# Attention by blocks of sixteen query columns in a two-layer diffusion trunk

## The chip, the cores and the metric

The kernel runs on one core of one Trainium2 chip. The metric is the device time of one execution in microseconds; for the kernel before it is the median of three runs. One execution was also taken by the hardware profiler, and the views quoted below come from that one.

## What is computed

The reference is a two-layer trunk over 256 latent tokens (a grid of 4 rows and 64 columns) with 256 context tokens, width 1024. What matters here is the attention of each layer, with 8 heads of 64 channels:

```python
# per latent query at grid column c, all 4 rows are in reach (kh = min(8, rows) = 4)
col_start = jnp.clip(cols - 8, 0, 64 - 16)          # a window of 16 columns
s_win = q . k_window * scale + bias                 # 4 x 16 = 64 window keys
s_ctx = q . k_ctx * scale                           # 256 context keys
p = softmax(concat([s_win, s_ctx]))                 # one softmax over both
out = p_win @ v_window + p_ctx @ v_ctx
```

So a latent query sees 64 of the 256 latent keys, and all 256 context keys. q and k are turned by a rotary table first. Context tokens attend to context only, in the first layer; the last layer needs only their keys and values. The rest of a layer is an input projection (convolution branch, q/k/v, gates), a depthwise convolution of 31 taps, output projections and a gated MLP with 2816 channels.

## The kernel before

**Products.** Activations are held with channels on the 128 partitions and tokens along the free axis: 256 latent tokens, then 256 context tokens (slices `LAT`, `CTX`). A weight unit of 128 x 1024 floats comes from HBM by a DMA that SP issues (`raw_unit`, L146; tag `raw`, four buffers). It is split into a high and a low fp32r half: ACT casts the high half (L161), and DVE subtracts for the low half (L162); for the units in `ADDED`, ACT makes the high half and its negative (L199, L200) and a DMA that GpSimd issues adds the raw unit to it (L201). A product is then three fp32r matmuls (`mm3`, L180 to L182). A *group* is one output tile of 128 channels: 8 input chunks times three matmuls of 512 columns in layer 0 and of 256 in layer 1.

**Attention.** Layer 0 first makes V for its four token tiles of 128 (`v_tile`, L683) and copies each from its PSUM bank (L816); layer 1 does so in two halves (L832). Then `qk(j)` (L788) makes one pair of heads: a group for q, the bias by a DMA (L799), the rotary in four DVE steps (L801 to L804), and the split into high and low halves by an ACT and a DVE step for latent and context part (L807, L808); then the same for k. The class `Attention` queues the work of a pair: two query tiles of 128 tokens, and in layer 0 one context item for every two pairs. A pair goes through three steps, each run when the side work has had its turns between groups (`step`, L430):

1. scores (`products`, L467): for each query tile three terms on the two halves of the partitions (one head each), against all 512 keys, into the banks `sc`, `sc` and `pt`, `main`; then (`scores`, L476) DVE adds the bias and takes the maximum in one pass (L483), ACT takes the exponential with its sum (L486), DVE the reciprocal (L488), ACT scales (L489). Keys outside the window have a bias of -1e30.
2. turning (`turn`, L511): TensorE transposes the probabilities in pieces of 64 queries by 128 keys (L520), and ACT copies them from PSUM (L523; L526 for context).
3. values (`values`, L530): fp32 matmuls of V with the turned probabilities, four key tiles of 128 for latent queries (L538), and the split of the result (L544, L545).

The order on each engine is that in which the program asks for the work, as the scheduler of the language then places it; every engine, and SP with the weight DMAs, works its own queue in order. The 31 taps of the convolution (L625, DVE) run as side work between groups, so many at each turn (`rate`). Scratch tiles (`tmp`, L70) come from a ring of five. PSUM has four banks `main`, two `sc`, one `pt`, one `po`.

Of the kernel before, what the change touches and what calls it, by code (L numbers as in the profile page):

```python
# [8 lines left out]
F32 = mybir.dt.float32  # L9
# [6 lines left out]
P = 128  # L16
# [30 lines left out]
def trunk(ctx: ExitStack, tc: tile.TileContext, xt, cvec, crow, wall, wada, params, bias_t, rope_t, out):  # L47
# [348 lines left out]
    class Attention:  # L396

        def __init__(self, l, eb, T, V, oh, ol, after):  # L400
            self.after = after
            self.l, self.eb, self.T, self.V, self.oh, self.ol = l, eb, T, V, oh, ol
# [64 lines left out]
        def products(self, it, out):  # L467
            j, qt, q, k, bt = it
            if qt is not None:
                self.product(out, q, k, slice(qt * P, (qt + 1) * P), slice(0, 2 * S))  # L470
            else:
                for t in range(2):
                    self.product([ps[:, t * S : (t + 1) * S] for ps in out], q, k, slice(S + t * P, S + (t + 1) * P), CTX)
            return out

        def scores(self, it, out):  # L476
            qt, bt = it[1], it[-1]
            pps = []
            for i, ps in enumerate(out):

                mx = small([P, 1], "mx")
                p2, b2 = ps.rearrange("p (a k) -> p a k", a=2), bt[:, 2 * qt + i :: 4 - 2 * qt - i, :]
                self.after[0] = dve.tensor_tensor_reduce(p2, p2, b2, -1.0, 3.0e38, ALU.add, ALU.min, mx)  # L483
                pp = self.eb.tile([P, 512], F32, tag="pp", bufs=4, name=nm("pp"))
# [3 lines left out]
                dve.reciprocal(ri, sm)  # L488
                self.done = act.mul(pp, pp, ri)  # L489
                pps.append(pp)  # L490
            return pps
# [19 lines left out]
        def turn(self, what, its, pps):  # L511

            pT = self.eb.tile([P, 2, 4, S], F32, tag="pT", bufs=2, name=nm("pT"))
            for n, tags in enumerate((("sc", "sc"), ("pt", "main"))):
                outs = [psum(t).rearrange("p (i s q) -> p i s q", i=2, s=4) for t in tags]
                for i, pp in enumerate(pps[n]):
                    for s in range(4):
                        src = s if what == LAT else s % 2 * 2 + s // 2
                        for pt, r in zip(outs, HALF):
                            pe.transpose(pt[:, i, s], sl(pp, src)[r], ident[r, r])  # L520
                for pt, r in zip(outs, HALF):
                    if what == LAT:
                        self.copied = act.copy(pT[:, :, :, n * P + r.start : n * P + r.stop], pt)  # L523
                    else:
                        to = pT[:, :, 2 * n : 2 * n + 2].rearrange("p i k (t q) -> p i (k t) q", t=2)
                        self.copied = act.copy(to[:, :, :, r], pt)  # L526
            js = [its[0][0]] if what == LAT else [it[0] for it in its]
            self.pv.append((what, js, [pT[:, i] for i in range(2)]))

        def values(self, what, js, pT, bank):  # L530
            po = psum(bank)
            kts = range(4) if what == LAT else range(2, 4)
            for n, j in enumerate(js):
                c = slice(n * S, (n + 1) * S)
                for kt in kts:
                    for i in range(2):
                        h = 2 * j + i
                        pe.matmul(  # L538
                            po[i * HD : (i + 1) * HD, c], self.V[kt][:, h * HD : (h + 1) * HD],
                            pT[i][:, 2 * n + kt - kts[0]], start=kt == kts[0], stop=kt == kts[-1],  # L540
                        )
            for n, j in enumerate(js):
                c = slice(n * S, (n + 1) * S)
                act.copy(self.oh[j][:, what], po[:, c])  # L544
                dve.tensor_tensor(self.ol[j][:, what], po[:, c], self.oh[j][:, what].bitcast(F32), ALU.subtract)  # L545

    sums0 = psum("pt")

# [33 lines left out]
    for l in range(DEPTH):  # L584
# [5 lines left out]
        with ExitStack() if last else start as e1a:  # L590
# [80 lines left out]

            with ExitStack() as e1b:
                eb = e1b.enter_context(tc.tile_pool(name=f"eb{l}", bufs=1))
                V = [eb.tile([P, CONV], F32, name=f"V{l}_{t}") for t in range(4)]
                att = Attention(l, eb, T, V, oh, ol, after)

                def v_tile(pv, w, k, toks, parts=range(3)):
                    i = k % 2
# [109 lines left out]
                def qk(j):  # L788

                    att.ahead(j - 2)  # L790
                    bt = eb.tile([P, 5, S], F32, tag="bias", bufs=2 if last else 1, name=nm("bias"))
                    both = []
                    for what in range(2):
                        w = T if what == 0 else 2 * S
                        sc = HD ** -0.5 if what == 0 else 1.0
                        ps = in_group((T_Q, T_K)[what] + j, slice(0, w))
                        if what == 0:
                            with tc.issue_after(lastdma[0].ins):
                                sp.dma_start(bt, bias_t[l, j])  # L799
                        r1, r2 = tmp(), tmp()  # L800
                        dve.tensor_tensor(r1[:, LAT], ps[:, LAT], rope[:, 0, :], ALU.mult)  # L801
                        dve.stream_shuffle(r2[:, LAT], ps[:, LAT], SWAP16)
                        dve.tensor_tensor(r2[:, LAT], r2[:, LAT], rope[:, 1, :], ALU.mult)
                        dve.tensor_tensor(r1[:, LAT], r1[:, LAT], r2[:, LAT], ALU.add)  # L804
                        f = eb.tile([P, 2, w], F32R, tag="qk"[what], bufs=2, name=nm("qk"))
                        for src, c in ((r1, LAT), (ps, CTX))[: w // S]:
                            act.activation(f[:, 0, c], src[:, c], AF.Identity, scale=sc)  # L807
                            end = dve.scalar_tensor_tensor(  # L808
                                f[:, 1, c], src[:, c], sc, f[:, 0, c].bitcast(F32), ALU.mult, ALU.subtract
                            )  # L810
                        both.append(f)
                    att.pair(j, *both, bt, end)

                if l == 0:
                    for t in range(4):
                        act.copy(V[t], pv[t])  # L816
                    qk(0)
                    arun = att.run()
                    add_side(arun)
                    for j in range(1, 4):  # L820
                        glu_groups(j)
                        qk(j)
                else:
                    wvs = [wunit(l, U_V + uu) for uu in range(4)]
                    for half in range(2):
                        pv = {t: psum() for t in (2 * half, 2 * half + 1)}
                        for k in range(KD):
                            v_tile(pv, wvs[k // 2], k, pv)
                            if k % 2:
                                slot()  # L830
                        for t, p in pv.items():
                            act.copy(V[t], p)  # L832
# [368 lines left out]
def _bias_layout(rpb):  # L1201

    import numpy as np

    c = np.arange(GW)
    start = np.clip(c - 8, 0, GW - 16)
    kc = np.arange(GW)
    inside = (kc[None] >= start[:, None]) & (kc[None] < start[:, None] + 16)
    at = np.where(inside, kc[None] - c[:, None] + 15, 0)
    t = rpb[:, :, 4:11][:, :, :, at]  # L1210
    t = np.where(inside, t, np.float32(MASKED))
    t = t.transpose(0, 3, 1, 2, 4).reshape(DEPTH, GW, HEADS, 7 * GW)
    rows = [t[:, :, :, (3 - r) * GW : (7 - r) * GW] for r in range(4)]

    b = np.stack(rows, axis=1).reshape(DEPTH, 2, P, 4, 2, S).transpose(0, 3, 2, 1, 4, 5).reshape(DEPTH, 4, P, 4, S)
    return np.concatenate([b, np.zeros((DEPTH, 4, P, 1, S), np.float32)], axis=3)


# [46 lines left out]
```

## Time and profile before

| what | value |
|---|---|
| median of 3 runs | 1124.99 us (1124.82 to 1125.58) |
| profiled execution | 1124.46 us, its span 1122.7 us, granted TensorE clock 0.998 |
| attention in layer 0, first score product to last value product | 82 to 197 us |
| attention in layer 1 | 795 to 864 us |
| L520, transposes | 320 matmul records |
| L538, value products | 160 records |
| L465, score products | 96 of 512 columns (latent), 48 of 256 (context) |
| HBM read | 188.62 MB |

How to read it: the page gives each engine's busy time and its share of the span, the span in 40 slices of 28 us, and the chain of work that ended last. A line such as L538 is a line of the kernel. Groups give the count, the total busy time, the mean of one in ns, and what ended the idle time before them. PE is the matmul, PEld the load of its stationary operand, DVE, ACT and POOL the vector, scalar and GpSimd engines, SPq the queue that issues the DMAs. A matmul's own duration includes its way through the array, and matmuls overlap: what one costs is the distance from its start to the start of the next.

### The profile page before, as it was taken

To read this page: it belongs to the slowest core of one execution; us is meant where nothing else is said; L and a number is where in the kernel's file an instruction comes from. 1 tells how busy PE (TensorE), PEld (TensorE's weight loads), DVE (VectorE), ACT (ScalarE), POOL (GpSimd) and SP (SyncE) were. 2 spreads that over 40 slices of the span, in tenths; PEclk is the share of its full clock that TensorE was granted. 3 is DMA by queue.
4 is the path that set the end of the run, shared out by engine and by line. 5 is a ranking of instruction groups with operands and counts; after the bars stand their busy time and mean duration, and the time that the engine had idled before them with its cause. 6 is when DMAs were issued, how large, how long until landed. Compare 5 with 4: busy or idle time off the path is not lost.

```text
span 1122.7 us, 18139 instructions
## 1 busy us (share of the span) xinstructions
PE 1110.2 (99%) x6988; PEld 955.8 (85%) x6988; DVE 887.7 (79%) x1607; ACT 588.9 (52%) x960; POOL 36.5 (3%) x50
## 2 busy tenths in 40 slices
PE   9999999999999999999999999999999999999997
PEld 7777777787789988888888888989888999999997
DVE  5579799875878788888888555789699898988773
ACT  4468878541333543434433223545777657766642
POOL 1011110000000000000000000000100000000000
PEclk9999999999999999999999999999999999999999
DMA  9988572544744354554556656557854575666781
GB/s 362 290 191 216 137 174 62 196 154 171 249 132 126 115 154 150 169 171 149 169 171 211 222 182 194 184 182 195 224 167 138 156 242 171 188 194 183 220 269 57
DMA packets 57687, 204.49 MB, mean 182 GB/s; under 512 B 6656, under 2 KB 6912, under 8 KB 57600
## 3 DMA queue, kind: packets, MB, share of 16 engines
q1 hardware_dynamic: 53568, 189.65, 53.1%
q0 software_dynamic: 3744, 13.63, 6.4%
q8 instruction: 55, 0.90, 0.3%
q14 instruction: 32, 0.26, 0.1%
q10 hardware_dynamic: 288, 0.04, 0.0%
HBM read 188.62 MB, written 1.05 MB: 169 GB/s over the span
## 4 chain that ended last, share of the span: by engine, by line
PE 88%; issue 5%; DVE 4%; ACT 2%; POOL 0%; POOLq 0%; DVEq 0%; ACTq 0%
PE main L180 25%; PE main L182 25%; PE main L181 25%; PE main L683 4%; DVE cb L625 2%; PE po L538 1%; PE sc L182 1%; PE sc L180 1%; PE sc L181 1%; PE po L213 1%; PE sc L465 1%; PE sc L130 1%; PE sc L213 0%; PE pt L465 0%; PE sc L520 0%
## 5 line engine op out<-in xcount | busy, mean ns | idle before, releaser
L180 PE MATMUL main<-h,whi 128*128 128x256 f32 (+1 forms) x1328 | 446.7, 337 | 0.0
L182 PE MATMUL main<-h,wlo 128*128 128x256 f32 (+1 forms) x1328 | 442.9, 335 | 1.0 <-DVE wlo L162 1.0
L181 PE MATMUL main<-h,whi 128*128 128x256 f32 (+1 forms) x1328 | 442.3, 334 | 0.1
L161 ACT CAST whi<-raw 128x1024 fp32r<-128x1024 f32 (+1 forms) x218 | 225.3, 1037 | 256.6 <-DMA raw<-in_wall 137.4
L162 DVE TENSOR_TENSOR wlo<-raw,whi 128x1024 fp32r<-128x1024 f32 (+1 forms) x218 | 262.2, 1208 | 98.9 <-ACT whi L161 96.9
L180 PEld LDWEIGHTS main<-h,whi 128*128 128x128 f32 x1328 | 249.4, 188 | 32.2 <-issue 4.3
L182 PEld LDWEIGHTS main<-h,wlo 128*128 128x128 f32 x1328 | 249.3, 188 | 29.6 <-DVE wlo L162 1.5
L181 PEld LDWEIGHTS main<-h,whi 128*128 128x128 f32 x1328 | 249.8, 188 | 28.6 <-DVE h L378 0.5
L625 DVE SCALAR_TENSOR_TENSOR cb<-u,par,cb 128x512 f32<-128x512 f32 (+1 forms) x240 | 144.2, 614 | 3.2
L282 DVE CUSTOM_DVE_ANT_0 t<-raw,sb,par 128x1024 bf16<-128x1024 f32 x100 | 126.6, 1277 | 1.3 <-DMA raw<-in_wada 1.3
L180 PE MATMUL main<-fh,whi 128*128 128x256 f32 (+1 forms) x386 | 123.0, 319 | 0.0
L181 PE MATMUL main<-fl,whi 128*128 128x256 f32 (+1 forms) x386 | 123.0, 319 | 0.0
L182 PE MATMUL main<-fh,wlo 128*128 128x256 f32 (+1 forms) x386 | 122.9, 318 | 0.0
L182 PEld LDWEIGHTS main<-fh,wlo 128*128 128x128 f32 x386 | 72.7, 188 | 5.6
L181 PEld LDWEIGHTS main<-fl,whi 128*128 128x128 f32 x386 | 72.7, 188 | 5.6
L180 PEld LDWEIGHTS main<-fh,whi 128*128 128x128 f32 x386 | 72.7, 188 | 5.5
L1003 ACT ACTIVATE t<-main,par 128x512 f32<-128x512 f32 (+1 forms) x82 | 50.7, 668 | 37.4 <-PE main L182 37.4
L1004 DVE SCALAR_TENSOR_TENSOR t<-main,par,t 128x510 f32<-128x510 f32 (+1 forms) x82 | 47.5, 615 | 9.5 <-ACT t L1003 9.1
L1007 DVE SCALAR_TENSOR_TENSOR t<-main,par,t 128x510 f32<-128x510 f32 (+1 forms) x82 | 46.6, 609 | 0.0
L377 ACT ACTIVATE h<-t,mod 128x256 fp32r<-128x256 f32 x56 | 25.5, 502 | 37.4 <-DVE t L376 37.2
L683 PE MATMUL main<-whi,h 128*128 128x512 f32 x128 | 40.6, 402 | 0.1
L1029 ACT CAST fh<-t 128x256 fp32r<-128x256 f32 (+1 forms) x43 | 21.9, 510 | 34.9 <-DVE t L1019 34.5
(220 smaller groups left out, 1266.2 us busy)
## 6 DMA issues: line engine op xcount, KB each, us to landing
raw<-in_wall SPq DMA_DIRECT2D x239, 512.0 KB, 4.2
raw<-in_wada SPq DMA_DIRECT2D x88, 512.0 KB, 4.4
wlo<-raw POOLq DMA_DIRECT2D x26, 512.0 KB, 5.6
bias<-in_bias_t SPq DMA_DIRECT2D x8, 640.0 KB, 4.7
row<-in_wada SPq DMA_DIRECT2D x8, 512.0 KB, 4.9
sb<-in_crow SPq DMA_DIRECT2D x5, 512.0 KB, 6.2
x<-in_xt SPq DMA_DIRECT2D x8, 256.0 KB, 4.4
raw<-in_wall SPq DMA_DIRECT2D x8, 256.0 KB, 7.7
```

Of the source, the lines that this page charges most:

```text
L161: act.copy(hi[:, c], r[:, c])
L162: dve.tensor_tensor(lo[:, c], r[:, c], hi[:, c].bitcast(F32), ALU.subtract)
L180: pe.matmul(ps, w[0], xh, start=start, stop=False)
L181: pe.matmul(ps, w[0], xl, start=False, stop=False)
L182: pe.matmul(ps, w[1], xh, start=False, stop=stop)
L282: dve.tensor_tensor_reduce(tmp().bitcast(BF16), r, v, 1.0, pr(l, BADA + n, 1), ALU.mult, ALU.add, mods[l][:, n, s : s + 1])
L377: high = act.activation(hi[:, c], y[:, c], AF.Identity, bias=b)
L625: dve.scalar_tensor_tensor(cb[j], src, w, cb[j], ALU.mult, ALU.add)
L683: mm = pe.matmul(pv[t], h1[n == 1][k][:, c], w[n == 2][:, b], start=k + n == 0, stop=k == KD - 1 and n == 2)
L1003: act.activation(c, pv_, AF.Identity, bias=pr(l, FDB + t, 1), scale=w[1])
L1004: dve.scalar_tensor_tensor(c[:, :, 1:], pv_[:, :, : S - 1], w[0], c[:, :, 1:], ALU.mult, ALU.add)
L1007: dve.scalar_tensor_tensor(c[:, :, : S - 1], pv_[:, :, 1:], w[2], c[:, :, : S - 1], ALU.mult, ALU.add)
```

## The change

The queries of a layer are put in another order: four blocks of sixteen grid columns, each with its four rows (64 queries). A block's windows lie within 32 columns of the grid (from column 0, 8, 24 and 32), that is 128 latent keys for 64 queries. A query tile holds two blocks; the windows of the two lie within 40 columns, 160 latent keys.

- *Scores* are taken on 160 latent and 256 context keys, 416 columns for 512. k is laid out as [latent of grid columns 24 to 63 | context 256 | latent of grid columns 0 to 39], 160 + 256 + 160 = 576 columns, each latent piece with the four rows of a grid column side by side, so that tile 0 reads the last 416 columns and tile 1 the first 416. The latent part of k is therefore split in two pieces of 160 columns (they overlap by 64 of 256 tokens), each written with a stride of four floats. q takes the block order in its rotary add, which now writes a further scratch tile. The bias has 2.5 x 416 columns in place of 2.5 x 512.
- *Turning* has three key slices for four: one with the 128 latent keys of the block at hand, two of context. The copy from PSUM moves 384 columns for 512.
- *Values* take the two context tiles over all 256 queries as before, and then for each block and head one product of the block's 128 latent keys with its 64 queries. For that V is kept a second way: the two latent tiles are copied into scratch, and eight DMAs for each, issued by SP, spread 32 rows of 512 floats into `VW`, one set of 128 keys for each block.
- The output is put back into the old order by the views of its two last steps.

The diff, cut to its core:

```diff
+ROWS = S // GW
+NB_, BC = 4, 16
+WC, TC = 32, 40
+BASE = (0, 8, 24, 32)
+KL, KX, KN = ROWS * TC, ROWS * TC + S, 2 * ROWS * TC + S
+KCTX = slice(KL, KX)
+NS_ = KL + S
...
             if qt is not None:
-                self.product(out, q, k, slice(qt * P, (qt + 1) * P), slice(0, 2 * S))
+                d = slice(0, NS_) if qt else slice(KL, KN)
+                self.product([ps[:, :NS_] for ps in out], q, k, slice(qt * P, (qt + 1) * P), d)
...
-                outs = [psum(t).rearrange("p (i s q) -> p i s q", i=2, s=4) for t in tags]
+                ns = 3 if what == LAT else 4
+                outs = [psum(t)[:, : ns * P].rearrange("p (i s q) -> p i s q", i=2, s=ns) for t in tags]
...
+                            elif s:
+                                off = (KL if n else 0) + (s - 1) * P
+                                src = pp[r, off : off + P]
+                            else:
+                                off = (0 if n else S) + 8 * ROWS * b
+                                src = pp[r, off : off + P]
+                            pe.transpose(pt[:, i, s], src, ident[r, r])
...
+                for b in range(NB_ if what == LAT else 0):
+                    q = slice(b * HD, (b + 1) * HD)
+                    for i in range(2):
+                        h = 2 * j + i
+                        pe.matmul(
+                            po[i * HD : (i + 1) * HD, q], self.VW[:, b, h * HD : (h + 1) * HD],
+                            pT[i][:, 0, q], start=False, stop=b == NB_ - 1, skip_group_check=True,
+                        )
...
-                V = [eb.tile([P, CONV], F32, name=f"V{l}_{t}") for t in range(4)]
+                V = [eb.tile([P, CONV], F32, name=f"V{l}_{t}") for t in range(2)]
+                VW = eb.tile([P, NB_, CONV], F32, name=f"VW{l}")
+
+                def keep_v(t, ps):
+                    if t > 1:
+                        act.copy(V[t - 2], ps)
+                        return
+                    v = tmp()
+                    act.copy(v, ps)
+                    for b in range(NB_):
+                        for r in range(2):
+                            at = r * GW + BASE[b]
+                            sp.dma_start(VW[2 * t + r :: ROWS, b], v[at : at + WC])
...
+                        if what == 0:
+                            rq = tmp()
+                            dve.tensor_tensor(
+                                rq[:, LAT].rearrange("p (b r c) -> p b r c", b=NB_, r=ROWS),
+                                blocks(r1[:, LAT]), blocks(r2[:, LAT]), ALU.add,
+                            )
...
+                            rv_ = r1[:, LAT].rearrange("p (r c) -> p r c", r=ROWS)
+                            to = [([f[:, a, KCTX] for a in range(2)], ps[:, CTX])]
+                            for d, c in ((slice(0, KL), slice(GW - TC, GW)), (slice(KX, KN), slice(0, TC))):
+                                to.append(([f[:, a, d].rearrange("p (c r) -> p r c", r=ROWS) for a in range(2)], rv_[:, :, c]))
+                        for (hi, lo), src in to:
+                            act.activation(hi, src, AF.Identity, scale=sc)
+                            end = dve.scalar_tensor_tensor(lo, src, sc, hi.bitcast(F32), ALU.mult, ALU.subtract)
```

More of the change, by code (lines that the diff above doesn't have):

```diff
@@ L469, in products @@
             if qt is not None:
-                self.product(out, q, k, slice(qt * P, (qt + 1) * P), slice(0, 2 * S))
+                d = slice(0, NS_) if qt else slice(KL, KN)
+                self.product([ps[:, :NS_] for ps in out], q, k, slice(qt * P, (qt + 1) * P), d)
             else:
                 for t in range(2):
-                    self.product([ps[:, t * S : (t + 1) * S] for ps in out], q, k, slice(S + t * P, S + (t + 1) * P), CTX)
+                    self.product([ps[:, t * S : (t + 1) * S] for ps in out], q, k, slice(S + t * P, S + (t + 1) * P), KCTX)
             return out
@@ L531, in values @@
             po = psum(bank)
-            kts = range(4) if what == LAT else range(2, 4)
             for n, j in enumerate(js):
                 c = slice(n * S, (n + 1) * S)
-                for kt in kts:
+                for kt in range(2):
                     for i in range(2):
@@ L543, in values, with blocks @@
                 c = slice(n * S, (n + 1) * S)
-                act.copy(self.oh[j][:, what], po[:, c])
-                dve.tensor_tensor(self.ol[j][:, what], po[:, c], self.oh[j][:, what].bitcast(F32), ALU.subtract)
+                to = [blocks(t[j][:, LAT]) if what == LAT else t[j][:, CTX] for t in (self.oh, self.ol)]
+                src = po[:, c].rearrange("p (b r c) -> p b r c", b=NB_, r=ROWS) if what == LAT else po[:, c]
+                act.copy(to[0], src)
+                dve.tensor_tensor(to[1], src, to[0].bitcast(F32), ALU.subtract)
+    def blocks(ap):
+        return ap.rearrange("p (r b c) -> p b r c", r=ROWS, b=NB_)
     sums0 = psum("pt")
@@ L790, in qk @@
                     att.ahead(j - 2)
-                    bt = eb.tile([P, 5, S], F32, tag="bias", bufs=2 if last else 1, name=nm("bias"))
+                    bt = eb.tile([P, 5, NS_ // 2], F32, tag="bias", bufs=2 if last else 1, name=nm("bias"))
                     both = []
@@ L815, in trunk @@
                     for t in range(4):
-                        act.copy(V[t], pv[t])
+                        keep_v(t, pv[t])
                     qk(0)
@@ L831, in trunk @@
                         for t, p in pv.items():
-                            act.copy(V[t], p)
+                            keep_v(t, p)
                     glu_groups(2)
@@ L1211, in _bias_layout @@
     t = np.where(inside, t, np.float32(MASKED))
[L1212 to L1216, printed above, removed]
+    p = np.arange(P)
+    kr = np.arange(ROWS)
+    half = NS_ // 2
+    b = np.zeros((DEPTH, 4, P, 5, half), np.float32)
+    for qt in range(2):
+        c = 32 * qt + 16 * (p // 64) + p % 16
+        r = p % 64 // 16
+        keys = np.arange(TC) + (GW - TC) * qt
+        w = t[:, :, kr[None, None, :] + 3 - r[:, None, None], c[:, None, None], keys[None, :, None]]
+        w = w.reshape(DEPTH, 4, 2, P, KL)
+        for i in range(2):
+            if qt:
+                b[:, :, :, i, :KL] = w[:, :, i]
+            else:
+                b[:, :, :, 3 + i, half - KL :] = w[:, :, i]
+    return b
 def kernel(**inputs):
```

39 lines of the change are left out of this document (22 added, 17 removed).

## The prediction

> **What bounds the kernel now.** I read the page first: the share of each engine, the slices, the chain that ended last.
>
> ```profile
> PE 1110.2 (99%) x6988; PEld 955.8 (85%) x6988; DVE 887.7 (79%) x1607; ACT 588.9 (52%) x960; POOL 36.5 (3%) x50
> ...
> PE   9999999999999999999999999999999999999997
> PE 88%; issue 5%; DVE 4%; ACT 2%; POOL 0%; POOLq 0%; DVEq 0%; ACTq 0%
> ```
>
> TensorE (PE) is busy in every slice, and the chain is 88% PE. A busy PE need not be a fast PE, so I then read the stretches in which attention runs, layer 0 (71 to 200 us) and layer 1 (742 to 865 us), by windows.
>
> ```profile
> 71.00:112.00 41.00, 40.87 (x244) 31.61 (x244) 40.07 (x87) 29.95 (x50) 5.20 (x6) 1.00 0.90 220
> 112.00:130.00 18.00, 17.74 (x97) 14.02 (x94) 12.40 (x30) 17.42 (x39) 1.84 (x3) 1.00 0.37 91
> 130.00:200.00 70.00, 70.00 (x474) 52.97 (x476) 65.41 (x125) 52.99 (x104) 5.11 (x6) 1.00 0.54 133
> 742.00:765.00 23.00, 23.00 (x104) 18.70 (x104) 22.93 (x52) 10.45 (x17) 0.00 (x0) 1.00 0.41 123
> 825.00:865.00 40.00, 40.00 (x385) 35.05 (x382) 37.35 (x82) 34.75 (x74) 1.57 (x1) 1.00 0.39 115
> ```
>
> Columns after the length: busy us of PE, weight load, DVE, ACT, POOL; clock, DMA share, GB/s. PE is full at clock 1.00, but DVE is nearly full too (40.07 of 41, 22.93 of 23) and ACT is in one stretch (17.42 of 18). So the question is whether PE ever waits for them here. The list of waits, and one place of it in the PE timeline:
>
> ```profile
> PEld sc L465 <- ACT pT L523: 3.9, 8, 1.2
> PE sc L465 <- ACT pT L523: 1.0, 2, 0.8
> ```
>
> Score products wait for the copy that empties the turned probabilities from the two "sc" banks; PE itself lost 1.0 us so, and the weight loads 3.9 us ahead of it, in part under running matmuls. That is little against eight turns. I take attention as PE-bound, and what PE no longer does as time saved, less what these waits take back.
>
> **The change, part by part.** There are eight head pairs, four in each layer, each with two query tiles, one turn and one value product. Context attention of layer 0 keeps its size.
>
> *PE work.* The PE timeline of one turn and its values; of the transposes the first and the last of eight rows on "pt" (each has a twin on the other row half, started with it):
>
> ```profile
> 132.77 0.22 PE L520 MATMUL pt<-ident,pp 64*128 64x64 f32 x1
> ...
> 133.20 0.22 PE L520 MATMUL pt<-ident,pp 64*128 64x64 f32 x1
> ...
> 133.36 1.95 PE L538 MATMUL po<-pT,V 128*64 128x256 f32 x16
> ```
>
> Seven steps take 0.43 us, so a pair of transposes costs 0.061 us. A turn goes from 32 transposes to 24 (three key slices for four), four pairs fewer: 0.25 us a head pair. For values, the row holds 16 records for 8 products (each fp32 product makes two passes). They too run in pairs, on the two column halves: 8 pairs in 1.95 us, less the last one's own 0.38 (L538's mean is 385 ns) over seven steps: 0.22 a pair. The latent half, 4 pairs or 0.88 us, goes. In its place come 4 blocks x 2 heads x 2 passes = 16 records, 8 pairs of 64 columns. The trace has none of that shape. From below, 64/256 of 0.22 is 0.055 a pair; nothing excludes that except a fixed part, which would only add. From above, the weight loads set the pace, by the nearest row in which almost nothing is streamed (one column, 128 columns of fp32 weights):
>
> ```profile
> 221.76 0.78 PE pt L347 x8
> ```
>
> That is 0.098 us for 128 weight columns, 0.049 for 64; one after another, 0.098 a pair. I take 0.061, the transposes' pace, the one row with 64 streamed columns, whose two loads ran under the products. So 8 x 0.061 = 0.49 comes, 0.88 goes: 0.39 saved (ends 0.10 and 0.44). [...]
>
> Scores lose 96 of 512 columns. Two stretches of plain products give the price of a column, at 512 and at 256 columns:
>
> ```profile
> 980.00:1100.00 120.00, 120.00 (x1016) 120.00 (x1015) 96.53 (x150) 71.18 (x109) 0.00 (x0) 1.00 0.68 208
> 742.00:764.00 22.00, 22.00 (x96) 17.75 (x96) 21.93 (x49) 9.45 (x16) 0.00 (x0) 1.00 0.39 121
> ```
>
> 118 ns at 256 and 229 ns at 512: 0.43 ns a column, 0.042 us for 96. Scores run in pairs on row halves, 3 terms x 2 tiles = 6 pairs: 0.25 us.
>
> PE sum: 0.25 + 0.39 + 0.25 = 0.89 a head pair, times eight 7.1 us (ends 4.8 and 7.5).
>
> *DVE and ACT.* Six rows picked from the groups by shape price the rest (mean ns behind the comma):
>
> ```profile
> L1004 DVE SCALAR_TENSOR_TENSOR t<-main,par,t 128x510 f32<-128x510 f32 x42 | 29.6, 745 | 8.4 <-ACT t L1003 8.2
> L1004 DVE SCALAR_TENSOR_TENSOR t<-main,par,t 128x255 f32<-128x255 f32 x40 | 17.9, 478 | 1.1 <-ACT t L1003 0.8
> L808 DVE SCALAR_TENSOR_TENSOR qk<-t,qk 128x256 fp32r<-128x256 f32 x16 | 6.7, 419 | 1.0 <-ACT qk L807 1.0
> L489 ACT ACTIVATE pp<-pp,ri 128x512 f32<-128x512 f32 x32 | 21.8, 720 | 0.2 <-DVE ri L488 0.2
> L507 ACT ACTIVATE pp<-pp,ri 128x256 f32<-128x256 f32 x16 | 7.2, 520 | 0.0
> L807 ACT ACTIVATE qk<-t 128x256 fp32r<-128x256 f32 x16 | 6.7, 419 | 14.7 <-DVE t L804 14.7
> ```
>
> DVE pays 1.05 ns a column (745 and 478), ACT 0.78 (720 and 520). DVE: four bias-and-maximum passes lose 96 columns, -0.40 us; the latent keys are split into two pieces of 160 columns for one of 256, 2 x 0.32 - 0.42 = +0.22. Net -0.18 a head pair. ACT: four exponentials and four scalings -0.60, four copies of turned blocks lose 128 columns -0.40, the second key piece +0.27. Net -0.73. The query add through a block view, the output through one and the fewer bias bytes I count as nothing: same elements, under PE. If the cover went, the key pieces would cost PE about 0.5 us a head pair. [...]
>
> *V.* Two of the four V copies go into scratch and then through 16 transfers of 64 KB a layer, on SP, which also issues every weight load. Each waits for its copy, and the loads behind it wait too. ACT's copies and a cast behind them; SP's loads around them (two windows); POOL's accumulation that makes a low half, and its time to landing; the PE product that needs it; the page's row of loads; a wait of SP:
>
> ```profile
> 56.61 1.76 ACT L816 COPY V<-main 128x512 f32<-128x512 f32 x3 [0.94 <-PE main L683]
> 62.57 1.04 ACT L199 CAST whi<-raw 128x1024 fp32r<-128x1024 f32 x1
> ```
> ```profile
> 53.69 12.18 SPq L148 DMA_DIRECT2D raw<-in_wall  x3
> 65.54 0.33 SPq L148 DMA_DIRECT2D raw<-in_wall  x1
> ```
> ```profile
> 65.06 0.89 POOL L201 DMA_DIRECT2D wlo<-raw  x1 [3.14 <-ACT wlo L200]
> ```
> ```profile
> DMA to landing us min/median/max: 4.4/7.0/7.5
> ```
> ```profile
> 77.11 0.39 PE L182 MATMUL main<-h,wlo 128*128 128x512 f32 x1
> ```
> ```profile
> raw<-in_wall SPq DMA_DIRECT2D x239, 512.0 KB, 4.2
> ```
> ```profile
> SPq L148 <- DMA raw<-in_wall: 15.7, 7, 5.1
> ```
>
> An issue takes 0.33 us, so 16 take 5.3. SP also waits for earlier loads to land before it issues a further one (15.7 us in 7 times), so with many small transfers in the air the second half may wait a landing: up to 2 x 4.2 and some, 9.4 us as upper end. The copies are ready from 57.2; SP's three loads of 53.69 to 65.87 leave it mostly waiting in between, so 5.3 us fit ahead of the load at 65.54 if the two earlier ones go first. If they stand behind: the load of 53.69 goes at 66.6, 12.9 late. It has 4.7 us until its cast (lands about 57.9, cast 62.57), and the low half has 4.5 (issued 65.06, 7.5 at most, used 77.11): 9.2, so PE would lose 3.7. In layer 1:
>
> ```profile
> 752.49 1.29 ACT L832 COPY V<-main 128x512 f32<-128x512 f32 x2 [1.12 <-PE main L683]
> 764.16 1.05 ACT L161 CAST whi<-raw 128x1024 fp32r<-128x1024 f32 x1
> ```
> ```profile
> 746.56 15.13 SPq L158 DMA_DIRECT2D raw<-in_wall  x3
> 758.25 0.33 SPq L158 DMA_DIRECT2D raw<-in_wall  x1
> ```
> ```profile
> 767.21 0.28 PE L182 MATMUL main<-h,wlo 128*128 128x256 f32 x1
> ```
>
> Copies ready at 753.8, plus 5.3 is 759.1; at worst 763.2, 5 us late for the load of 758.25, which has 1.7 to its cast and about 0.8 behind: 2.5 lost. I take nothing for V (ends 0 and 6.2), since both gaps in SP's queue hold the plain 5.3 us almost whole. V's two scratch buffers come from the ring of five; with the sigmoid's and the rope's two it is full, and the query add takes the sigmoid's, which is free by then: no wait counted.
>
> *What is late next.* After its "sc" banks are filled, PE reaches the next score product 0.5 us sooner (half of the transposes' 0.25, and the values' 0.39), while the two copies that empty the banks are 0.2 us shorter. Where ACT is late already, 0.3 us a head pair is waited away: 2.4 over eight. Since the waits are few now, I take about half, 1.1 (ends 0 and 2). Sum: 7.1 - 1.1 = 6.0. The profiled execution took 1124.46 (span 1122.7 and 1.8 around it), 0.5 under the median; 1124.46 - 6.0 = 1118.5, on the median's footing **1119.0 us**.
>
> **Rivals.** (1) *Weight loads pace the block products* (0.098 a pair, 4.8 us in all) and the waits take 2: 1124.99 - 2.8 = 1122.2. For: the shape is new. Against: L538 and the transposes load under running products. (2) *Slower: V's transfers ahead of the weights in SP's queue*, decided where a load is over 9.2 us (layer 0) or 2.5 us (layer 1) late: 3.7 + 2.5, and in layer 0 their 1.05 MB are in the way of the accumulating transfers. By the DMA view of 50 to 115 us:
>
> ```profile
> q0 software_dynamic: 1610, 5.87, 48.2%
> ```
>
> 48.2% of 65 us for 5.87 MB is 5.3 us a MB, so 5.6 us of all engines where they are 90% busy. 11.8 - 6.0: 1131. For: DMA share 0.90. Against: the copies come in SP's gap. (3) *Nothing gained*: DVE, full in 71 to 112 and 742 to 765, holds the pace and PE waits for it; its own work falls by only 8 x 0.18 = 1.4 us: 1123.6 to 1125.0. Against: PE waits 1.0 us for those copies in all.
>
> **How the numbers follow.** Forecast 0.54, rival 1 0.20, rival 2 0.18, rival 3 0.08. A measurement tells about 0.2%, 2.25 us, from no change: rival 1 lies near that edge, so I give 0.14 of it to faster and 0.06 to the same. Faster 0.68, same 0.14, slower 0.18. From below, block pairs at 0.055 (7.5) and the waits gone with ACT's relief (another 2 to 3): 1114.5. From above, rivals 1 and 3, the ends of V and the near part of rival 2: 1128.
>
> **What would show it.** Right: L520's successor has 256 records for 320, scores 416 columns at some 0.19 us a pair, block values near 0.06 a pair, PE without gaps around 60 to 80 and 760 to 770. Wrong: block pairs near 0.1; waits on pT above 5 us; PE waiting for wlo or whi behind SP's V transfers; key pieces well over 0.35 us.

## The result and the profile after

The changed kernel takes 1121.13 us (median of 19 runs, 1119.41 to 1126.74) where the kernel before takes 1125.50 us (19 runs beside them). The ratio is 0.9966, 95% interval 0.9957 to 0.9975: 0.34% or 3.8 us faster. The forecast was 6.0 us. The profiled execution took 1121.22 us, 3.24 us under that of before. The page of the changed kernel first: busy time by engine, then the chain that ended last by engine.

```profile
PE 1103.7 (99%) x6988; PEld 954.0 (85%) x6988; DVE 886.9 (79%) x1615; ACT 582.8 (52%) x968; POOL 36.2 (3%) x50
...
PE 83%; DVE 7%; ACT 5%; DMA 3%; issue 1%; SPq 1%; DVEq 0%; ACTq 0%
```

TensorE is still at 99%, but the chain is 83% PE where it was 88%; DVE, ACT, DMA and SP's queue have grown in it. PE has been shortened and in part waits. The groups by shape, mean ns behind the comma:

```profile
L472 PE MATMUL sc<-qk,qk 64*128 64x416 f32 x48 | 7.8, 391 | 2.4 <-ACT pT L544 0.8 <-ACT qk L864 0.7 <-DVE qk L865 0.5
L564 PE MATMUL po<-pT,VW 128*64 128x64 f32 x128 | 5.1, 222 | 0.0
...
L865 DVE SCALAR_TENSOR_TENSOR qk<-t,qk 128x160 fp32r<-128x160 f32 x16 | 6.8, 458 | 0.2 <-ACT qk L864 0.2
L864 ACT ACTIVATE qk<-t 128x160 fp32r<-128x160 f32 x16 | 6.6, 504 | 6.9 <-DVE t L852 6.9
```

L472 is the score product: PE waited 2.4 us ahead of its "sc" forms, half of it for the keys (qk), which it never did before. L564 is the new block product. L864 and L865 write the key pieces: 504 and 458 ns where I had taken 0.34 and 0.32 us. The end of a turn (a context turn, which keeps its 32 transposes), the values of a latent pair behind it, and the end of one score step, from the PE timeline ("..." leaves rows out):

```profile
134.24 0.22 PE L538 MATMUL pt<-ident,pp 64*128 64x64 f32 x1
134.30 0.22 PE L538 MATMUL main<-ident,pp 64*128 64x64 f32 x1
...
134.58 1.08 PE L555 MATMUL po<-pT,V 128*64 128x256 f32 x8
135.49 0.64 PE L564 MATMUL po<-pT,VW 128*64 128x64 f32 x16
```
```profile
164.73 0.35 PE L472 MATMUL pt<-qk,qk 64*128 64x416 f32 x1
164.92 0.35 PE L472 MATMUL pt<-qk,qk 64*128 64x416 f32 x1
165.11 0.35 PE L472 MATMUL pt<-qk,qk 64*128 64x416 f32 x1
```

The transposes keep their 0.06 us a pair. The values now end 1.55 us after their start (134.58 to 136.13) for 1.95 before; the eight block pairs start within 0.64 - 0.22 = 0.42 us, 0.06 a pair. A score pair takes 0.19 us.

**Where the gain is, and where not.** Every PE product outside attention is there in both kernels, from 60 us on in the same order, so one and the same product can be looked up in both traces, and the difference of its two starts tells how far the changed kernel is ahead (negative) at that place:

| product at, in the kernel before | 78.04 us | 198.16 us | 740.06 us | 870.07 us | 1115.42 us |
|---|---|---|---|---|---|
| changed kernel against before, us | +0.99 | -0.10 | +0.62 | -2.89 | -3.18 |

Attention of layer 0 (second column less the first) gains 1.09 us, that of layer 1 (fourth less third) 3.51. The 0.99 at the start and the 0.72 between the layers arise outside attention (at 9 to 13 us, and near 617 us, where PE waits for a low half of weights). They differ from one profiled execution to the next: the other kernels below with block attention stand between 0.31 us ahead and 0.65 behind there at the start, and all but e10 lose 0.3 to 1.2 us between the layers; the kernel of e2, whose attention is the old one, loses nothing there. So layer 1 gave all that was forecast, 4 x 0.89 = 3.6, and layer 0 a third of it. What stands in layer 0's way shows in SP's queue and in ACT's:

```profile
64.41 14.59 SPq L716 DMA_DIRECT2D VW<-t  x16
79.11 1.98 SPq L155 DMA_DIRECT2D raw<-in_wall  x4
```
```profile
63.31 0.60 ACT L672 ACTIVATE t<-sc 128x512 f32<-128x512 f32 x1
63.81 1.07 ACT L712 COPY t<-main 128x512 f32<-128x512 f32 x2
...
75.72 0.80 ACT L864 ACTIVATE qk<-t 128x160 fp32r<-128x160 f32 x2 [1.27 <-DVE t L852]
83.29 1.05 ACT L206 CAST whi<-raw 128x1024 fp32r<-128x1024 f32 x1 [6.78 <-DMA raw<-in_wall]
...
89.28 0.61 ACT L496 ACTIVATE pp<-sc,mx 128x416 f32<-128x416 f32 x1
```

The two V copies into scratch (L712) run only at 63.81, behind the sigmoid (L672), where before all four were done by 59.8. SP stands at the first transfer and waits 6.6 us for these copies. The sixteen transfers hold SP from 64.41 to 79.00, and the next weight load goes at 79.11; before it went at 65.54. ACT, which works in order, waits 6.78 us for that load, and the first exponential comes at 89.28 (86.00 before). In the kernel before:

```profile
86.00 0.69 ACT L486 ACTIVATE pp<-sc,mx 128x512 f32<-128x512 f32 x1
```

PE pays a little later, most of it at the second head pair's scores:

```profile
103.52 0.45 PE L472 MATMUL sc<-qk,qk 64*128 64x416 f32 x2 [0.75 <-ACT qk L864]
104.43 0.65 PE L472 MATMUL sc<-qk,qk 64*128 64x416 f32 x4 [0.46 <-DVE qk L865]
```

Product by product against e5 below, 1.55 us of the 2.4 are lost up to the end of these scores, and 0.8 at the turn and the scores behind them, up to 116 us.

### The profile page after: what moved, and what is told of

It reads as the page before. It is cut to its first block, busy times and chain, and to the rows that moved or that the text cites. A ratio compares the mean times of both kernels' runs of the same rounds, so it can differ in the third digit from the quotient of the medians.

```text
span 1119.4 us, 18214 instructions
## 1 busy us (share of the span) xinstructions
PE 1103.7 (99%) x6988; PEld 954.0 (85%) x6988; DVE 886.9 (79%) x1615; ACT 582.8 (52%) x968; POOL 36.2 (3%) x50
## 4 chain that ended last, share of the span: by engine, by line
PE 83%; DVE 7%; ACT 5%; DMA 3%; issue 1%; SPq 1%; DVEq 0%; ACTq 0%
PE main L187 24%; PE main L189 24%; PE main L188 24%; PE main L724 4%; DMA raw<-in_wall 2%; DVE cb L654 2%; SPq L716 1%; DVE wlo L169 1%; PE sc L187 1%; PE sc L189 1%; PE sc L188 1%; PE po L555 1%; ACT whi L168 1%; PE po L220 1%; DMA x<-in_xt 1%
```

## The experiments

The theories. **1**: the V transfers, in SP's queue ahead of the weights, make a load late, ACT waits for it, and layer 0 loses about 2.5 us. **2**: the key pieces, written one float per 16 bytes, make the keys late. **3**: DVE and ACT hold the pace of layer 0 in any case, and what PE saves it waits. "Layer 0" and "layer 1" below are gains between the same products as in the table above.

| kernel | us (median) | ratio to before, 95% | layer 0 | layer 1 |
|---|---|---|---|---|
| changed kernel | 1121.13 | 0.9966 (0.9957 to 0.9975) | -1.09 | -3.51 |
| e1 no transfers | 1122.50 | 0.9970 (0.9958 to 0.9982) | -3.47 | -0.62 |
| e2 before + transfers | 1124.82 | 0.9998 (0.9989 to 1.0006) | 0.00 | 0.00 |
| e3 plain keys | 1120.20 | 0.9954 (0.9942 to 0.9966) | -1.69 | -3.88 |
| e4 later transfers | 1119.23 | 0.9953 (0.9940 to 0.9965) | -3.50 | -3.52 |
| e5 own V tiles | 1117.98 | 0.9937 (0.9925 to 0.9949) | -3.49 | -3.53 |
| e6 strided read | 1118.78 | 0.9954 (0.9939 to 0.9968) | -3.35 | +1.50 |
| e7 none in layer 0 | 1119.33 | 0.9946 (0.9933 to 0.9959) | -3.49 | -2.03 |
| e8 keys in the add | 1118.56 | 0.9940 (0.9927 to 0.9954) | -3.68 | -3.88 |
| e9 doubled in layer 0 | 1124.16 | 0.9990 (0.9981 to 0.9999) | +2.21 | -3.49 |
| e10 = e5 again | 1118.74 | 0.9948 (0.9935 to 0.9960) | -3.46 | -1.99 |

The times are from many runs, the columns on the layers from one profiled execution each; where they differ, it is layer 1 (see e10) and the stretch between the layers that vary. A diff below is cut to its core; those of e6, e8 and e9 are shown against the kernel of e5, the others against the changed kernel, and e2 against the kernel before.

**e1: no transfers**

```diff
+                pool.memset(VW, 0.0)
...
-                            sp.dma_start(VW[2 * t + r :: ROWS, b], v[at : at + WC])
```

> The changed kernel without the sixteen V transfers of each layer: VW is set to zero once by GpSimd, so the latent values are left out of the sums; the copies of V into scratch and all products stay. Theory 1 (the transfers, issued by SP ahead of the weight loads, hold up layer 0): about 2.5 us less than the changed kernel, about 1118.5 us where that takes 1121.1, the load behind them goes at about 66 us in place of 79, and ACT no longer waits 6.8 us for it; layer 1 the same. Theory 2 (the key pieces, written one float per 16 bytes, make the keys late): as the changed kernel within 0.5 us. Theory 3 (DVE and ACT hold the pace in layer 0 in any case): as the changed kernel within 0.5 us, and PE's waits only move to other places.

Layer 0 gained 3.47 us, as theory 1 said and against 2 and 3. But the time did not fall. Layer 1 of the profiled execution gained only 0.62: ACT waited 4.6 us there for one weight load, PE 1.3 and 0.8 us for ACT, and then PE's clock went down (see the last section). Whether that happened in all five runs (1120.33 to 1123.07 us) no profile shows, so as a test of the whole time this one is inconclusive.

**e2: the kernel before, with the transfers**

```diff
+                def keep_v(t, ps):
+                    act.copy(V[t], ps)
+                    for b, base in enumerate((0, 8, 24, 32) if t < 2 else ()):
+                        for r in range(2):
+                            at = r * GW + base
+                            sp.dma_start(VW[2 * t + r :: 4, b], V[t][at : at + 32])
```

> The kernel before with the sixteen V transfers of each layer added on SP, into a tile that nothing reads; attention stays as it was. Theory 1: 1.5 to 2.5 us more than the kernel before, nearly all of it between 75 and 200 us. Theory 2 and theory 3: as the kernel before within 0.5 us.

Nothing: theory 1 as it stood fell. SP's queue in this kernel:

```profile
58.14 14.38 SPq L682 DMA_DIRECT2D VW<-V  x16
72.64 14.40 SPq L148 DMA_DIRECT2D raw<-in_wall  x5
```

The transfers take as long as in the changed kernel, but they start at 58.14 in place of 64.41; here V goes into tiles of its own, and ACT copies it early. The load behind them is 7.1 us late (72.64 for 65.54), and no product starts later for it. So the new form of theory 1: not the transfers as such, but transfers that start late, because the copies wait for scratch.

**e3: plain keys**

```diff
-  to.append(([f[:, a, d].rearrange("p (c r) -> p r c", r=ROWS) for a in range(2)], rv_[:, :, c]))
+  to.append(([f[:, a, d].rearrange("p (r c) -> p r c", r=ROWS) for a in range(2)], rv_[:, :, c]))
```

> The changed kernel with the two latent key pieces written as four plain runs of 40 floats in place of one float per 16 bytes. The keys of a piece then stand in another order than the bias and V, so the output is not the reference's. Theory 2: the pieces fall from 458 (DVE) and 504 ns (ACT) to about 0.32 and 0.35 us, and the time by about 2 us against the changed kernel. Theory 1: the pieces may fall, but the time stays within 0.5 us, since the keys are late from the load on. Theory 3: between the two, up to 1 us less.

```profile
L864 ACT ACTIVATE qk<-t 128x160 fp32r<-128x160 f32 x16 | 4.7, 334 | 6.9 <-DVE t L852 6.9
L865 DVE SCALAR_TENSOR_TENSOR qk<-t,qk 128x160 fp32r<-128x160 f32 x16 | 4.6, 319 | 0.1
```

The pieces fell to what was expected, 334 and 319 ns: the stride cost 0.17 us on ACT and 0.14 on DVE a piece. The layers gained 0.6 and 0.4 us over the changed kernel, half of theory 2's figure. So the dear pieces are real, but they are the smaller part.

**e4: later transfers**

```diff
-                    v = tmp()
+                    v = eb.tile([P, CONV], F32, name=f"v{l}_{t}")
...
-                            sp.dma_start(VW[2 * t + r :: ROWS, b], v[at : at + WC])
+                            later.append((VW[2 * t + r :: ROWS, b], v[at : at + WC]))
...
+    def loaded():
+        if skip[0]:
+            skip[0] -= 1
+            return
+        for _ in range(min(4 if quarter[0] else 8, len(later))):
+            with tc.issue_after(lastdma[0].ins):
+                sp.dma_start(*later.pop(0))
...
         lastdma[0] = sp.dma_start(r, src)
+        loaded()
```

> The changed kernel with V in tiles of its own and the transfers of each layer issued behind later weight loads: layer 0 eight behind each of two loads of the GLU, layer 1 eight, four and four. Nothing else changes. Theory 1: about 2 us less than the changed kernel (1119 us), ACT's wait of 6.8 us at 76 to 83 us gone or under 2 us. Theory 2 and theory 3: as the changed kernel within 0.5 us. A rival within theory 1: the sixteen issues of 0.59 us cost the same wherever they stand, since SP is behind by 9.4 us either way; then it is as the changed kernel too, with another load late.

Layer 0 gained 3.50 us and layer 1 3.52. Theory 3 falls: DVE and ACT let all of it through. But this kernel changes two things, the tiles and the place in the queue; the next one changes the tiles alone.

**e5: own V tiles, the transfers where they were**

```diff
-                    v = tmp()
+                    v = eb.tile([P, CONV], F32, name=f"v{l}_{t}")
```

> The changed kernel with the two latent V tiles copied into tiles of their own in place of scratch from the ring; the transfers stay where they are in SP's queue, one for one. Theory 1 in its new form (the ring gives the copies their buffers only behind the sigmoid, so the transfers start at 64 us and hold the loads behind them; with early copies they fit into SP's gap): as the kernel with later transfers, about 2 us less than the changed kernel, layer 0 gains about 3.5 us over the kernel before, the load behind the transfers goes at about 66 to 70 us in place of 79. Theory 1 in its old form (the place in the queue alone is to blame): as the changed kernel, layer 0 gains about 1 us.

This one line gives layer 0 back in full, 3.49 us for 1.09, and the whole takes 1117.98 us, 0.63% under the kernel before. SP's queue is the same, transfer for transfer, as in the changed kernel; only its clock times differ. SP's and ACT's timelines:

```profile
58.10 12.79 SPq L716 DMA_DIRECT2D VW<-v  x16
71.01 15.57 SPq L155 DMA_DIRECT2D raw<-in_wall  x5
```
```profile
57.49 1.07 ACT L712 COPY v<-main 128x512 f32<-128x512 f32 x2 [0.94 <-PE main L724]
...
77.68 1.06 ACT L206 CAST whi<-raw 128x1024 fp32r<-128x1024 f32 x1 [1.51 <-DMA raw<-in_wall]
...
86.65 0.61 ACT L496 ACTIVATE pp<-sc,mx 128x416 f32<-128x416 f32 x1
```

The copies run at 57.49 in place of 63.81; the load goes at 71.01, still 5.5 us later than before, and ACT waits 1.51 us for it in place of 6.78. The first exponential comes at 86.65 for 89.28. A later place in the queue with the copies still in scratch was not run.

Not all of the gain lasts. Just behind the attention of layer 0, PE waits 0.49 us here for an ACT copy, since ACT had waited 2.45 us for a transfer of 512 KB (`in_crow`), and the lead over the kernel before falls from 2.84 to 2.19 us. In e7 PE waits 1.04 us there, in e10 not at all; e1, e4, e6 and e8 lose 0.3 to 0.9 us at this place. Why the transfer lands later in some executions is left open.

**e6: strided read**

```diff
-  to.append(([f[:, a, d].rearrange("p (c r) -> p r c", r=ROWS) for a in range(2)], rv_[:, :, c]))
+  to.append(([f[:, a, d].rearrange("p (c r) -> p c r", r=ROWS) for a in range(2)], rv_[:, :, c].rearrange("p r c -> p c r")))
```

> The kernel with own V tiles, and the key pieces besides written in order (160 floats side by side) while their source in scratch is read with a stride (four rows 256 bytes apart). If only writing one float per 16 bytes is dear, the pieces fall to about 0.32 (DVE) and 0.34 us (ACT) and the time by up to 1 us against the kernel with own V tiles; if reading so is as dear, the pieces stay near 0.46 and 0.50 us and the time stays.

```profile
L864 ACT ACTIVATE qk<-t 128x160 fp32r<-128x160 f32 x16 | 7.2, 497 | 6.0 <-DVE t L852 6.0
...
L865 DVE SCALAR_TENSOR_TENSOR qk<-t,qk 128x160 fp32r<-128x160 f32 x16 | 6.6, 439 | 0.2 <-ACT qk L864 0.2
```

Reading with the stride costs as much as writing with it (497 and 439 for 504 and 458 ns). Nothing is won so. The profiled execution lost time in layer 1, like e1's.

**e7: no transfers in layer 0 alone**

```diff
+                if not last:
+                    pool.memset(VW, 0.0)
...
+                            if last:
-                            sp.dma_start(VW[2 * t + r :: ROWS, b], v[at : at + WC])
+                                sp.dma_start(VW[2 * t + r :: ROWS, b], v[at : at + WC])
```

> The changed kernel without the sixteen V transfers of layer 0 alone: its VW is set to zero once by GpSimd, so layer 0's latent values are left out of the sums; the copies into scratch and layer 1 stay as they are. Theory 1: layer 0 gains about 3.5 us over the kernel before where the changed kernel gains 1, and layer 1 its 3.5, so about 2 us less than the changed kernel; if layer 1 loses some 2 to 3 us, as it did without all transfers, the loss there comes from layer 0's new pace and not from layer 1's own transfers. Theory 3: as the changed kernel.

1119.33 us, ratio 0.9946 for the changed kernel's 0.9966, and 3.49 us in layer 0 with the late copies still in scratch. The copies run at 62.53, late as in the changed kernel, in ACT's timeline:

```profile
62.53 1.07 ACT L714 COPY t<-main 128x512 f32<-128x512 f32 x2
```

So late copies alone do no harm, nor do transfers that follow early copies (e2, e5); late copies with the transfers behind them cost layer 0 its 2.4 us. The whole time points the same way, though the intervals of the two ratios overlap a little. Layer 1 lost 1.5 us in the profiled execution, though its transfers stood as in the changed kernel.

**e8: the keys turned in the add**

```diff
-                            dve.tensor_tensor(r1[:, LAT], r1[:, LAT], r2[:, LAT], ALU.add)
+                            rk = tmp()
+                            dve.tensor_tensor(
+                                rk[:, LAT].rearrange("p (c r) -> p r c", r=ROWS),
+                                r1[:, LAT].rearrange("p (r c) -> p r c", r=ROWS),
+                                r2[:, LAT].rearrange("p (r c) -> p r c", r=ROWS), ALU.add,
+                            )
...
+                            for d, c in ((slice(0, KL), ROWS * (GW - TC)), (slice(KX, KN), 0)):
+                                to.append(([f[:, a, d] for a in range(2)], rk[:, c : c + KL]))
```

> The kernel with own V tiles, and the latent keys besides put into block order once, by the last add of their rotary (into a scratch tile of its own, 256 floats written one per 16 bytes), so that both key pieces read and write side by side. Keys late (theory 2, what is left of it): the pieces fall to 0.32 (DVE) and 0.33 us (ACT), the add rises from 0.42 to about 0.64, DVE is even and ACT 0.34 us a head pair shorter, and the time falls by 0.3 to 1 us against own V tiles. Theory 3 in its weak form (nothing waits for the keys any more once V is early): as own V tiles within 0.3 us.

```profile
L853 DVE TENSOR_TENSOR t<-t,t 128x256 f32<-128x256 f32 x8 | 4.9, 614 | 0.0
L868 ACT ACTIVATE qk<-t 128x160 fp32r<-128x160 f32 x16 | 4.6, 330 | 7.2 <-DVE t L853 7.2
L869 DVE SCALAR_TENSOR_TENSOR qk<-t,qk 128x160 fp32r<-128x160 f32 x16 | 4.6, 321 | 0.1
```

The stride is paid once, in the add (614 for 0.42 us), and the pieces are cheap. The layers gain 0.2 and 0.35 us over e5 in the profiles. The times, 1118.56 and, beside it, 1118.74 us for own V tiles, can't tell them apart.

**e9: twice the transfers in layer 0**

```diff
+                if not last:
+                    VX = eb.tile([P, NB_, P], F32, name="VX")
...
                             sp.dma_start(VW[2 * t + r :: ROWS, b], v[at : at + WC])
+                            if not last:
+                                sp.dma_start(VX[2 * t + r :: ROWS, b], v[at : at + WC, :P])
```

> The kernel with own V tiles and sixteen further transfers in layer 0, one behind each of the sixteen, a quarter as wide, into a tile that nothing reads. Theory 1 (what counts is how late the load behind them goes): the load goes 10 to 13 us later than with own V tiles, at 81 to 84 us, 15 to 18 behind the kernel before; where 13.6 cost 2.4 us in the changed kernel and 5.5 nothing, this costs 4 to 7 us in layer 0, all of it at 75 to 115 us. If lateness of the load is not what cost the changed kernel its 2.4 us, it is as own V tiles.

```profile
57.85 0.53 SPq L718 DMA_DIRECT2D VW<-v  x1
58.43 0.58 SPq L720 DMA_DIRECT2D VX<-v  x1
...
83.00 0.59 SPq L720 DMA_DIRECT2D VX<-v  x1
83.70 11.52 SPq L155 DMA_DIRECT2D raw<-in_wall  x5
```
```profile
PE sc L472 <- ACT qk L868: 2.7, 1, 2.7
```

The copies are early here, and yet layer 0 ends 2.21 us behind the kernel before: 5.7 lost against e5. PE waits at the same score products for the same keys, now 2.7 us in one piece; behind that wait its granted clock falls to 0.51 (window of 107.0 to 110.5 us). How late the load goes against 65.54 us, less what the kernel's products were late at 78 us already (1.0 us in the changed kernel, 0.65 in e5, 0.35 in e9): 4.8 us (e5) costs nothing, 7.1 (e2, in the kernel before) nothing, 12.6 (changed kernel) 2.4, 17.8 (e9) 5.7. So the loss begins between 7.1 and 12.6 us of lateness. A straight line through the last two points (0.63 us of loss a us) would put the beginning at about 9 us (12.6 less 2.4 / 0.63), but that is a rough estimate: the fall of the clock, which the changed kernel does not have at this place, is part of e9's 5.7, and e9 also moves 0.26 MB more, which no run parts from the lateness.

**e10: own V tiles again**

The kernel of e5, unchanged.

> The kernel with own V tiles a second time, beside the two others on one chip: about 7 us under the kernel before, layer 0 and layer 1 each 3.4 to 3.6 us ahead; what differs from the first time lies at the start or in layer 1, where single loads land late.

Layer 0 as the first time (3.46), layer 1 only 1.99 for 3.53: one kernel, two executions, 1.5 us apart in one place. The windows of 809.00 to 812.50 us, first of e5, then of e10 (busy PE, PEld, DVE, ACT, POOL, then the granted clock):

```profile
809.00:812.50 3.50, 3.37 (x28) 3.10 (x29) 3.24 (x13) 3.50 (x10) 0.86 (x1) 1.00 0.62 179
```
```profile
809.00:812.50 3.50, 3.50 (x21) 3.34 (x20) 3.20 (x12) 3.50 (x10) 0.86 (x1) 0.66 0.78 224
```

The second ran at a clock of 0.66, so its loss in layer 1 belongs to the execution and not to the kernel. The profiled executions of e7 (0.51 in the same window), e1 and e6 (0.53 and 0.51 a few us later) have such a fall as well; in e1 and e6 a weight load that ACT waited 4.6 and 4.8 us for goes ahead of it. Why that load landed late is left open.

## Why the prediction was right, and where it was wrong

- **PE work: right.** 0.06 us a block pair, 0.19 a score pair, 256 transposes for 320, values 1.95 to 1.55 us. Where nothing else interferes, four head pairs gained 3.5 us (layer 1 of the changed kernel, e4, e5 and e9: 3.49 to 3.53; layer 0 of e1, e4, e5, e7 and e10: 3.46 to 3.50) for the 3.56 of the sum. Rival 1, weight loads that pace the block products, falls: they kept 0.06, not 0.098, which was an estimate from L347's pace (0.098 us for 128 weight columns), halved for 64 and taken for both loads.
- **V at nothing: this step failed.** It rested on "the copies are ready from 57.2" and on the ring of five with "no wait counted". In the changed kernel the two copies stood behind the sigmoid and ran at 63.81, so SP's gap had passed, and the transfers stood wholly ahead of the load of 65.54. That scratch from the ring makes them late is shown by e5; which use held the ring's buffers is not. An issue also took 0.59 us and not 0.33, and five of the sixteen took 0.94 to 1.81, so that together they took 14.6 us, more than my upper end of 9.4. I had reckoned with a wait for a landing there; SP's list of waits has none among the sixteen, the issues themselves were long, and why is open. Either alone should do no harm: with the early copies the long issue fits (e5); from 64.41 on, 5.3 us of issue would have put the load at 69.7, less late than e5's (no run tried that). The term measured 2.4 us, within its ends of 0 and 6.2.
- **Rival 2 was half right.** Its point of decision, a load over 9.2 us late in layer 0, lies between the 7.1 us that cost nothing and the 12.6 that cost 2.4, and the load came 13.6 us late by the clock, 12.6 by the kernel's own products. But its way was another: not PE waiting for the weights, but ACT in its order, and behind it the exponentials and the next keys. The loss was 2.4 us and not 3.7, layer 1 lost nothing, and of its third part, transfers in each other's way, nothing was needed to explain the loss.
- **Waits taken back, 1.1 us: too much.** Own V tiles gained 3.49 and 3.53 of 3.56 a layer: inside attention some 0.1 us went to waits, set against those that ended (with cheap keys, e3 and e8, a layer gained up to 3.88, more than the sum). Without V's cost the kernel gains 7.1 us by the medians (1125.07 to 1117.98; 6.4 the second time, e10). That this is the plain PE sum is partly chance: the profiled execution of e5 was 6.1 us ahead of that of before, with 0.65 lost at the start and 0.70 between the layers.
- **DVE and ACT: near by the page, but by luck.** By the page ACT's busy time fell by 588.9 - 582.8 = 6.1 us or 0.76 a head pair (0.73 forecast) and DVE's by 0.8 or 0.10 (0.18). But the page's busy time counts a stretch once where two instructions of an engine overlap, as ACT's L672 (63.31 to 63.91 us) and L712 (from 63.81) do in the changed kernel. By the rows (count times mean) ACT's exponentials, scalings and copies lost 1.06 us a head pair, near the 1.00 forecast, but the key pieces added 0.59 in place of 0.27: 0.47 less, not 0.73. DVE's bias passes lost 0.39 (0.40), but the pieces added 0.50 in place of 0.22: DVE has 0.11 more to do, not 0.18 less. So the key pieces were dearer than taken, on DVE by 0.28 us a head pair: 458 ns a piece, 319 without the stride (e3). What they cost in time, by one profiled execution each, is 0.2 us in layer 0 once V is early (e8) and 0.6 while it is late (e3), and 0.35 to 0.37 in layer 1.
- **Rival 3 falls.** DVE, full in the windows, let all of PE's gain through in e4 and e5. That the convolution's taps among its work can slip would explain it; that was not tried.
- In sum: 7.1 of PE work less 2.4 for V less 0.1 for waits is 4.6 us, which is what attention gained in the profiled execution (1.09 + 3.51). Outside attention that execution lost 0.99 and 0.72 and gained 0.29, which leaves 3.2; the runs gave 3.8 by the ratio and 4.4 by the medians. That the time fell well inside the range owes something to luck: V was taken 2.4 us too low and the waits 1.0 too high, so that the errors offset each other in part.

## What to carry to other kernels

When a step moves into another buffer pool, look up on its engine when the pool gives the buffer, not when the data is there: here a scratch ring in place of a tile of its own moved two copies by 6 us, and with them sixteen DMAs in front of a weight load. Count small DMAs by the time that they hold the issuing queue, and ask how late the next load may be: here 7 us cost nothing and 12.6 us cost 2.4. And compare the same product in both traces at several places: the total said that some 60% of the forecast had come, the table that one layer had given all of its share.

## What the runs showed of the hardware

- An issue of a transfer of 32 x 512 floats from SBUF to SBUF took 0.59 us of SP's time (478 to 1806 ns, median 599, in layer 0 of the changed kernel), a quarter as wide as long (579 to 1181, median 594, e9), where a load of 128 x 1024 floats takes 0.33 (median, kernel before). Between these two widths the width made no difference (medians of 596 and 594 ns, e9).
- Reading four floats 256 bytes apart cost ACT and DVE about as much as writing one float per 16 bytes (497 and 439 ns in e6, 504 and 458 in the changed kernel; 334 and 319 without either, e3).
- PE's granted clock fell for some us behind waits, short ones too, in e10 and not in e5, two executions of one kernel. In e1, after waits of 1.25 and 0.78 us at 808 to 810 us:

```profile
811.50:813.60 2.10, 2.10 (x11) 1.97 (x10) 1.82 (x9) 2.10 (x6) 0.86 (x1) 0.53 0.89 267
813.60:816.00 2.40, 2.40 (x23) 2.40 (x22) 2.33 (x8) 2.39 (x8) 0.00 (x0) 1.00 0.98 270
```

Eleven matmuls in 2.10 us at a clock of 0.53, then 23 in 2.40. In e9 the fall follows a wait of 2.7 us (0.51 from 107.0 to 110.5 us). In e10 the clock is 0.87 from 805.0 to 809.0 us, 0.66 to 812.5 and 1.00 to 817.0; two score pairs start 0.34 us apart there at 808.34 us (0.19 in e5), and products of 256 columns 0.21 apart up to 811.25 us and 0.12 from 811.44 on (0.12 in e5). In e5 and e10 the waits at that place were the same (0.4 and 0.6 us), and only e10's clock fell. What decided between the two no run here shows.
